# Decoder trunk with RWKV-7 mixing: the 16x16 eliminations go from VectorE to GpSimd, and each chain's blocks travel in 6 transfers instead of 20

## The chip, the cores and the metric

The kernel runs on 1 core of one Trainium2 chip. The metric is the device time of one execution in microseconds; of the kernel before there are three timed runs (median 1921.83, 1918.63 to 1923.67) and one profiled execution. A difference of about 0.3% is the least that a measurement of this kernel can tell from none.

## The reference, cut to what matters

Two layers; each layer is a SwiGLU feed-forward half step, a mixing step and another feed-forward half step. The mixing step concatenates sliding-window attention, RWKV-7 time mixing (4 heads of 64) and a short convolution. The part that matters here is the recurrence of RWKV-7 over 512 positions:

```python
def step(S, inp):
    r_t, w_t, k_t, v_t, kk_t, a_t = inp
    s_kk = jnp.einsum('bhvk,bhk->bhv', S, kk_t)
    S = (S * w_t[:, :, None, :] - s_kk[..., None] * (kk_t * a_t)[:, :, None, :]
         + v_t[..., None] * k_t[:, :, None, :])
    return S, jnp.einsum('bhvk,bhk->bhv', S, r_t)
```

## The kernel before, in words

Weights and activations are split into a high and a low half (`wH`/`wL`, `hnH`/`hnL`), and each large product is three matmuls. A weight tile is loaded through the SyncE queue (`wraw<-in_...`), cast on ScalarE (L101, `wH`) and subtracted on VectorE (L102, `wL`).

`mix` runs three things beside each other. `products` is the stream of projections `wmi` and then `wmo`, matmuls `ps_mm` at L98. `attention` is one generator. `rwkv(q)` is another, run for q = 0 and 1, two heads each; I call each run a chain, so there are four: two in each of the two layers. The loop at the end of `mix` takes product steps in between by the costs that the generators yield. The tile framework then orders the instructions of each engine from its own estimate of times; what it writes is fixed before the run, and each engine works its list strictly in order. So an instruction whose input is late holds back all that stands behind it on that engine.

Inside a chain the recurrence is computed in chunks of 64 positions. `pairs` makes `B` (matmuls `ps_c` at L824, mask on VectorE at L828). From `B`'s lower triangles the chain needs the inverse of 16 unit triangular 64x64 matrices (8 chunks, 2 heads). It is made in stages:

- The matrices are written to DRAM (`dl`, three transfers, L836 and L838), and the 64 diagonal blocks of 16x16 are read back with one block in each partition (`G`, eight transfers, L848).
- GpSimd sets `V_` (`inv`) to identity matrices (L850, L851). Then 15 elimination steps follow, each a product (L855, `elim`) and a difference (L856, `inv`) on VectorE: 30 instructions in a row that each need the one before, over 64 partitions and 15 to 64 elements of each (680 elements for the 15 products, and as many for the differences).
- The result goes to DRAM (`di`, one transfer, L858) and comes back spread over 128 partitions (`C`, eight transfers, L861).
- VectorE makes the block diagonal `T` from `C` (L915). TensorE transposes it (`ps_T`, L884), ScalarE copies that (`TT`, L919), and two levels of `ps_x`, `X` (L928), `ps_t` and `ps_tt` join the blocks to 64x64. Then come `ps_w`, `ps_gn` with `GT` and `N` (L965, L966) and the start state `St` (L969), `ps_o`, six sequential steps `ps_s` (L989, `St` at L990), `ps_ys`, `ps_v` and `ps_g`.

All transfers of a chain are issued from SyncE's queue, the one that also issues the weight loads, and it is worked in order too. GpSimd's queue holds the loads `wada` and the accumulating loads of the feed-forward parts; in `mix` it has nothing but memsets.

Of the kernel before, what the change touches and what calls it, by code (L numbers as in the profile page):

```python
# [8 lines left out]
F32 = mybir.dt.float32  # L9
# [3 lines left out]
ALU = mybir.AluOpType  # L13
# [3 lines left out]
P = 128  # L17
# [8 lines left out]
NB = T // P  # L26
CH = 64
NC = T // CH
HB = math.exp(-0.5) / 2
BASE = 16  # L30
# [27 lines left out]
def trunk_kernel(ctx, tc, ins, out, layers=L, phases=("ffn1", "mix", "ffn2")):  # L58
    nc = tc.nc
# [10 lines left out]
    dram = ctx.enter_context(tc.tile_pool(name="dram", bufs=1, space=bass.MemoryType.DRAM))  # L70
    tt, stt, ts = nc.vector.tensor_tensor, nc.vector.scalar_tensor_tensor, nc.vector.tensor_scalar
# [38 lines left out]
    rows = (slice(0, CH), slice(CH, P))  # L110
# [7 lines left out]
    for i in range(KD):  # L118
        t = hp_.tile([P, T], F32, name=f"h{i}")
# [15 lines left out]
    for name, v in (("eps", EPS), ("eps64", 64 * EPS), ("gneps", GN_EPS), ("nhb", -HB)):  # L135
        t = const.tile([P, 1], F32, name=f"v_{name}")
# [7 lines left out]
    def cst(name):  # L144
        a, b = CON[name]
        return con[:, a:b]
# [61 lines left out]
    def square(i, sl):  # L208
        sq = E("sq")[:, sl]
        act(sq, h[i][:, sl], AF.Square)  # L210
        return sq
# [373 lines left out]
    def mix(l, hn, ss, mp, then, ready):  # L585
# [5 lines left out]
        def pair(name):  # L591
            return rows_of(name != "y4", (name + "H", name + "L"))

        def S(q, name, shape=(P, T)):
            return mp.tile(list(shape), F32, name=f"{name}{q}", tag=f"s{q}", bufs=8)
# [4 lines left out]
        def EQ(q, name):  # L600
            return mp.tile([P, T], F32, name=name, tag=f"e{q}", bufs=2)
# [154 lines left out]
        def rwkv(q):  # L756
# [38 lines left out]
            t = EQ(q, "k2")  # L795
# [36 lines left out]
            B_, other = yield from pairs(be, "B", other)  # L832
            LT = B_[:, :, :, 0]

            dl = dram.tile([P, 2 * NB, CH], F32, name="dl", tag=f"dl{q}", bufs=2)
            nc.sync.dma_start(dl[rows[0]], LT[rows[0]].rearrange("p e b t -> p (e b) t"))  # L836
            for e in range(2):
                nc.sync.dma_start(dl[rows[1], (1 - e) * NB : (2 - e) * NB], LT[rows[1], e])  # L838
            NM = CH // BASE
            NT = 2 * NM * 2 * NB  # L840
            square = lambda t: t[:NT, : BASE * BASE].rearrange("p (t u) -> p t u", u=BASE)
            G = square(EQ(q, "G"))
            for c in range(2):
                for m in range(NM):
                    n = (c * NM + m) * 2 * NB
                    p0 = c * CH + m * BASE
                    src = dl[p0 : p0 + BASE, :, m * BASE : (m + 1) * BASE]
                    nc.sync.dma_start(G[n : n + 2 * NB], src.rearrange("r n t -> n r t"))  # L848
            V_ = square(EQ(q, "inv"))
            nc.gpsimd.memset(V_, 0.0)  # L850
            nc.gpsimd.memset(V_.rearrange("p t u -> p (t u)")[:, :: BASE + 1], 1.0)  # L851
            for s in range(BASE - 1):
                n = BASE - 1 - s
                t = mp.tile([NT, BASE * BASE // 4], F32, name="elim", tag=f"el{q}")[:, : n * (s + 1)].rearrange("p (t u) -> p t u", u=s + 1)
                tt(t, G[:, s, s + 1 :].unsqueeze(2).to_broadcast([NT, n, s + 1]), V_[:, s : s + 1, : s + 1].to_broadcast([NT, n, s + 1]), ALU.mult)  # L855
                tt(V_[:, s + 1 :, : s + 1], V_[:, s + 1 :, : s + 1], t, ALU.subtract)  # L856
            di = dram.tile([2 * NM, 2 * NB, BASE, BASE], F32, name="di", tag=f"di{q}", bufs=2)
            nc.sync.dma_start(di.rearrange("m n t u -> (m n) t u"), V_)  # L858
            C_ = EQ(q, "C")[:, : 2 * NB * BASE].rearrange("p (n u) -> p n u", u=BASE)
            for m in range(2 * NM):  # L860
                nc.sync.dma_start(C_[m * BASE : (m + 1) * BASE], di[m].rearrange("n t u -> t n u"))  # L861


            AX = U(q, "AX", [P, 2, NB, 2, CH])
# [48 lines left out]
            T4 = T_.rearrange("p e b (m u) -> p (e b) m u", u=BASE)  # L913
            msk = cst("diag").rearrange("p (m u) -> p m u", u=BASE).unsqueeze(1).to_broadcast([P, 2 * NB, NM, BASE])
            tt(T4, C_.unsqueeze(2).to_broadcast([P, 2 * NB, NM, BASE]), msk, ALU.mult)  # L915
# [39 lines left out]
            with tc.manual_schedule(engines={mybir.EngineType.PE}):  # L955
                for b in range(NB):
                    for c, e in ce:
                        m = mm(pgs[c][rows[e], 0, b], Wn[rows[c], c ^ e, b, :CH], beN[rows[c], b, rows[e]], start=True, stop=True)
# [12 lines left out]
            y = S(q, "y")  # L971
            pos = [psum([P, 2, NB, CH], "ps_o", R) for _ in range(2)]
            with tc.manual_schedule(engines={mybir.EngineType.PE}):
                for b in range(NB):
                    for c, e in ce:
                        m = mm(pos[c][rows[e], 0, b], Wn[rows[c], c ^ e, b, :CH], B_[rows[c], e, b, 1], start=True, stop=True)
# [116 lines left out]

        prod = products()
        live, waiting = {}, {"rwkv0": lambda: rwkv(0), "rwkv1": lambda: rwkv(1), "att": attention}
        left, fill, credit = 2 * RWKV_WORK + ATT_WORK, FILL_WORK, 0.0
        more = True
# [28 lines left out]
        for q in range(2):  # L1126
            x = pair("yr")
# [256 lines left out]
```

## Time and profile before

| what | value |
|---|---|
| median of 3 timed runs | 1921.83 us |
| profiled execution, its own time | 1921.27 us |
| its span in the profile | 1919.3 us |
| PE (TensorE matmul) busy | 1876.9 us, 98% |
| DVE (VectorE) busy | 1395.9 us, 73% |
| ACT (ScalarE) busy | 847.0 us, 44% |
| POOL (GpSimd) busy | 130.7 us, 7% |
| elimination steps on DVE | 60 and 60 instructions, 11.4 and 11.4 us busy |

Times in the trace are in microseconds from the start of the span. The first layer's mixing stands between about 435 and 620, the second layer's between about 1375 and 1560; an instruction of the second layer's mixing comes about 941.3 us after its twin of the first layer (the first `dl` store starts at 476.66 and at 1417.98). In a row of the timeline the first two numbers are start and duration, and the brackets at its end say how long the engine had been idle and what ended that. "SPq" is the time that SyncE's queue takes to issue transfers, not the transfers themselves. Matmuls of float32 stand twice in the trace and once in the orders below.

### The profile page before, as it was taken

The page shows a single profiled execution, that of the slowest core. Times are in us where ns is not written, and L with a number is a line of the kernel's source. Part 1 is how long each engine was busy: PE and PEld are TensorE (multiplying, and loading weights), DVE is VectorE, ACT ScalarE, POOL GpSimd, SP SyncE. Part 2 cuts the span into 40 slices and gives each one's busy share as a digit, 9 for nine tenths or more (in the row PEclk, how much of TensorE's full clock was granted, in tenths as well). Part 3 has the DMA queues.
Part 4 walks back from the last instruction along what each step waited for, and adds up shares of the span by engine and source line. Part 5 has one row for each costly group of instructions (what it writes and reads, how often), then busy time and mean ns, then how long its engine had stood idle before and what let it go on. Part 6 is the DMA issues. An engine that isn't in the chain of part 4 may idle for free. (4 is left out here: it accounts for less than half of the span.)

```text
span 1919.3 us, 37594 instructions
## 1 busy us (share of the span) xinstructions
PE 1876.9 (98%) x15744; PEld 1737.6 (91%) x15744; DVE 1395.9 (73%) x2185; ACT 847.0 (44%) x1292; POOL 130.7 (7%) x212
## 2 busy tenths in 40 slices
PE   8999999999999999999999999999998999999999
PEld 7998899987789999899899988989877899988998
DVE  7687687758966877677877776876598668873862
ACT  4443355356432554155345514544563335532551
POOL 0101101000000001110100020010000000110000
PEclk8999999999999999999999999999999999999999
DMA  7767877421312476887726687781211215764741
GB/s 299 252 163 228 261 195 241 153 69 47 86 39 75 124 196 181 272 218 200 259 79 179 169 272 227 197 276 44 89 55 49 87 34 156 213 213 134 197 139 59
DMA packets 104457, 308.50 MB, mean 161 GB/s; under 512 B 23520, under 2 KB 24544, under 8 KB 103264
## 3 DMA queue, kind: packets, MB, share of 16 engines
q1 hardware_dynamic: 76064, 203.33, 32.3%
q0 software_dynamic: 28224, 102.77, 21.5%
q8 instruction: 123, 2.02, 0.4%
q14 instruction: 46, 0.38, 0.1%
HBM read 302.66 MB, written 3.41 MB: 159 GB/s over the span
## 5 line engine op out<-in xcount | busy, mean ns | idle before, releaser
L101 ACT CAST wH<-wraw 128x1024 fp32r<-128x1024 f32 (+2 forms) x292 | 268.2, 922 | 512.0 <-PE ps_mm L91 162.0
L102 DVE TENSOR_TENSOR wL<-wraw,wH 128x1024 fp32r<-128x1024 f32 (+2 forms) x292 | 308.3, 1059 | 97.1 <-ACT wH L101 96.3
L90 PE MATMUL ps_mm<-actH,wH 128*128 128x512 f32 (+1 forms) x784 | 288.5, 368 | 0.0
L91 PE MATMUL ps_mm<-actL,wH 128*128 128x512 f32 (+1 forms) x784 | 288.0, 367 | 0.0
L92 PE MATMUL ps_mm<-actH,wL 128*128 128x512 f32 (+1 forms) x784 | 288.0, 367 | 0.0
L441 PE MATMUL ps_d<-comH,wH 128*128 128x256 f32 x816 | 226.7, 278 | 1.4 <-ACT wH L101 0.8
L443 PE MATMUL ps_d<-comH,wL 128*128 128x256 f32 x816 | 225.7, 277 | 2.3 <-DVE wL L102 2.3
L442 PE MATMUL ps_d<-comL,wH 128*128 128x256 f32 x816 | 225.4, 276 | 0.0
L98 PE MATMUL ps_mm<-hnH,wH 128*128 128x256 f32 x1040 | 215.9, 288 | 5.0 <-ACT hnH L101 2.9
L98 PE MATMUL ps_mm<-hnL,wH 128*128 128x256 f32 x1040 | 213.9, 284 | 0.0
L98 PE MATMUL ps_mm<-hnH,wL 128*128 128x256 f32 x1040 | 209.1, 282 | 0.5 <-DVE wL L102 0.5
L163 DVE SCALAR_TENSOR_TENSOR wada<-wada,crep 128x1024 f32<-128x1024 f32 x140 | 168.1, 1220 | 55.9 <-DMA wada<-in_wadaT 55.7
L102 DVE TENSOR_TENSOR wL<-sum,wH 128x1024 fp32r<-128x1024 f32 x102 | 124.9, 1224 | 73.7 <-ACT wH L101 73.6
L98 PEld LDWEIGHTS ps_mm<-hnH,wH 128*128 128x128 f32 x1040 | 160.8, 191 | 16.3 <-issue 7.9
L92 PEld LDWEIGHTS ps_mm<-actH,wL 128*128 128x128 f32 x784 | 147.8, 189 | 24.3
L91 PEld LDWEIGHTS ps_mm<-actL,wH 128*128 128x128 f32 x784 | 147.8, 189 | 24.2
L90 PEld LDWEIGHTS ps_mm<-actH,wH 128*128 128x128 f32 x784 | 147.8, 189 | 24.2
L98 PEld LDWEIGHTS ps_mm<-hnL,wH 128*128 128x128 f32 x1040 | 161.4, 191 | 7.1 <-issue 6.2
L101 ACT CAST wH<-sum 128x1024 fp32r<-128x1024 f32 x102 | 107.5, 1054 | 136.5 <-PE ps_d L442 60.1
L98 PEld LDWEIGHTS ps_mm<-hnH,wL 128*128 128x128 f32 x1040 | 160.2, 191 | 4.7 <-issue 3.4
L441 PEld LDWEIGHTS ps_d<-comH,wH 128*128 128x128 f32 x816 | 153.3, 188 | 3.5 <-ACT wH L101 1.4
L443 PEld LDWEIGHTS ps_d<-comH,wL 128*128 128x128 f32 x816 | 153.2, 188 | 2.9 <-DVE wL L102 2.9
(404 smaller groups left out, 4238.1 us busy)
## 6 DMA issues: line engine op xcount, KB each, us to landing
wada<-in_wadaT POOLq DMA_DIRECT2D x128, 512.0 KB, 4.9
wraw<-in_wmi SPq DMA_DIRECT2D x40, 512.0 KB
wraw<-in_w2p SPq DMA_DIRECT2D x36, 512.0 KB
wraw<-in_w1p SPq DMA_DIRECT2D x32, 512.0 KB
wraw<-in_w1o SPq DMA_DIRECT2D x32, 384.0 KB
wraw<-in_w2o SPq DMA_DIRECT2D x32, 384.0 KB
wraw<-in_w1i SPq DMA_DIRECT2D x20, 512.0 KB
wraw<-in_w1o SPq DMA_DIRECT2D x32, 320.0 KB
```

The lines of the kernel that those rows point to most:

```text
L90: mm(acc, wH, xH, start=start, stop=False)
L91: mm(acc, wH, xL, start=False, stop=False)
L92: mm(acc, wL, xH, start=False, stop=stop)
L98: mm(acc[:, sl], w[a][:, k], x[b][:, sl], start=start and n == 0 and sl is HALVES[0], stop=stop and n == 2, skip_group_check=True)
L101: nc.scalar.copy(hi, src)
L102: nc.vector.tensor_sub(lo, src, hi.bitcast(F32))
L163: stt(w, w, 1.0, crep, ALU.mult, ALU.mult, accum_out=out_)
L441: mm(pt[:, i], wH, x[k][0], start=start and i + k == 0, stop=False, skip_group_check=True)
L442: mm(pt[:, i], wH, x[k][1], start=False, stop=False, skip_group_check=True)
L443: last = mm(pt[:, i], wL, x[k][0], start=False, stop=k == 3, skip_group_check=True)
```

## The change

The 30 elimination instructions of each chain are issued on GpSimd instead of VectorE, with the same shapes. The layout of `dl` is changed so that all 64 blocks are read back into `G` by one transfer instead of eight, and that of `di` so that one transfer brings `C` instead of eight. The two memsets, the three `dl` stores and the `di` store stay. The new lines from L842 on are 4 or 5 lower than the old ones.

```diff
-            dl = dram.tile([P, 2 * NB, CH], F32, name="dl", tag=f"dl{q}", bufs=2)
-            nc.sync.dma_start(dl[rows[0]], LT[rows[0]].rearrange("p e b t -> p (e b) t"))
+            dl = dram.tile([2 * NB * 2, CH * CH + CH], F32, name="dl", tag=f"dl{q}", bufs=2)
+            dv = dl[:, : CH * CH].rearrange("(n c) (r t) -> c r n t", c=2, t=CH)
+            nc.sync.dma_start(dv[0], LT[rows[0]].rearrange("p e b t -> p (e b) t"))
             for e in range(2):
-                nc.sync.dma_start(dl[rows[1], (1 - e) * NB : (2 - e) * NB], LT[rows[1], e])
...
+                nc.sync.dma_start(dv[1][:, (1 - e) * NB : (2 - e) * NB], LT[rows[1], e])
             G = square(EQ(q, "G"))
-            for c in range(2):
-                for m in range(NM):
-                    n = (c * NM + m) * 2 * NB
-                    p0 = c * CH + m * BASE
-                    src = dl[p0 : p0 + BASE, :, m * BASE : (m + 1) * BASE]
-                    nc.sync.dma_start(G[n : n + 2 * NB], src.rearrange("r n t -> n r t"))
+            nc.sync.dma_start(G, dl.rearrange("x (m z) -> (x m) z", m=NM)[:, : BASE * CH].rearrange("y (r t) -> y r t", t=CH)[:, :, :BASE])
...
-                tt(t, G[:, s, s + 1 :].unsqueeze(2).to_broadcast([NT, n, s + 1]), V_[:, s : s + 1, : s + 1].to_broadcast([NT, n, s + 1]), ALU.mult)
-                tt(V_[:, s + 1 :, : s + 1], V_[:, s + 1 :, : s + 1], t, ALU.subtract)
-            di = dram.tile([2 * NM, 2 * NB, BASE, BASE], F32, name="di", tag=f"di{q}", bufs=2)
-            nc.sync.dma_start(di.rearrange("m n t u -> (m n) t u"), V_)
+                nc.gpsimd.tensor_tensor(t, G[:, s, s + 1 :].unsqueeze(2).to_broadcast([NT, n, s + 1]), V_[:, s : s + 1, : s + 1].to_broadcast([NT, n, s + 1]), ALU.mult)
+                nc.gpsimd.tensor_tensor(V_[:, s + 1 :, : s + 1], V_[:, s + 1 :, : s + 1], t, ALU.subtract)
+            di = dram.tile([2 * NB, 2 * NM, BASE, BASE], F32, name="di", tag=f"di{q}", bufs=2)
+            nc.sync.dma_start(di.rearrange("n m t u -> (n m) (t u)"), V_.rearrange("p t u -> p (t u)"))
             C_ = EQ(q, "C")[:, : 2 * NB * BASE].rearrange("p (n u) -> p n u", u=BASE)
-            for m in range(2 * NM):
-                nc.sync.dma_start(C_[m * BASE : (m + 1) * BASE], di[m].rearrange("n t u -> t n u"))
+            nc.sync.dma_start(C_, di.rearrange("n m t u -> (m t) n u"))
```

The framework orders everything around the chains anew. On TensorE, first layer, chain 0, before: the first `ps_T` stands among the `ps_c` of chain 1, long after `ps_kk` of chain 1.

```order
L824 MATMUL ps_c<-AR_6004,iP_5948 64x128 x9
L884 MATMUL ps_T<-con,T_5307 64x64 x16
L824 MATMUL ps_c<-AR_6004,iP_5948 64x128 x4
L884 MATMUL ps_x<-T_5307,B_5115 64x64
L824 MATMUL ps_c<-AR_6004,iP_5948 64x128
L884 MATMUL ps_x<-T_5307,B_5115 64x64 x15
L824 MATMUL ps_c<-AR_6004,iP_5948 64x128 x2
L869 MATMUL ps_vN<-con,v_5768 128x128 x4
```

The same place of the chain now: `ps_T` stands just ahead of `ps_kk` of chain 1, 21 products behind the last attention product `ps_av`.

```order
L98 MATMUL ps_mm<-hnL,wH 128x256 x2
L98 MATMUL ps_mm<-hnH,wL 128x256
L879 MATMUL ps_T<-con,T_5293 64x64 x16
L98 MATMUL ps_mm<-hnH,wL 128x256
L611 MATMUL ps_kk<-kksq,con 128x512
L879 MATMUL ps_x<-T_5293,B_5115 64x64 x16
L98 MATMUL ps_mm<-hnH,wH 128x256 x2
```

So `ps_T` of chain 0 has moved from the place that TensorE reached at 523.17 in the trace of before to the one just ahead of `ps_kk`, which it reached at 503.04. In the second layer it stands even earlier, directly behind that `ps_av`, without the 21 products.

On VectorE, first layer, before, around chain 1's reciprocal (L791): elimination steps of chain 0 alternate with other work.

```order
L855 TENSOR_TENSOR elim<-G,inv 64x60
L785 COPY pc_5943<-P_5934 128x8
L791 RECIPROCAL iP_5948<-P_5934 128x512
L856 TENSOR_TENSOR inv<-inv,elim 64x6x10
L635 SCALAR_TENSOR_TENSOR gd<-ps_mm,par,gd 128x511
L855 TENSOR_TENSOR elim<-G,inv 64x55
L788 TENSOR_SCALAR rn<-ps_kk 128x512
```

The same place now: `T`, which needs `C`, stands directly behind the reciprocal, ahead of a weight split.

```order
L785 COPY pc_5929<-P_5920 128x8
L791 RECIPROCAL iP_5934<-P_5920 128x512
L910 TENSOR_TENSOR T_5293<-C,con 128x512
L635 SCALAR_TENSOR_TENSOR gd<-ps_mm,par,gd 128x511
L810 TENSOR_TENSOR AR_5990<-r_5676,P_5920 128x512
L102 TENSOR_TENSOR wL<-wraw,wH 128x1024
```

The elimination is gone from VectorE, and what waits for `C` now holds back the rows below it. In the second layer `T` stands two scans (L783) ahead of the reciprocal.

SyncE's queue, second layer, before: `G` is read after one weight load, `di` and `C` much later.

```order
L838 DMA dl<-B_15845 64x4x64
L836 DMA dl<-B_15845 512x1x64
L838 DMA dl<-B_15845 64x4x64
L267 DMA wraw<-in_wmi 128x1024
L848 DMA G<-dl 8x16x16 x8
L267 DMA wraw<-in_wmi 128x1024 x2
L1010 DMA gw<-in_gw 128x256
L267 DMA wraw<-in_wmi 128x1024
L267 DMA wraw<-in_wmo 128x768
L858 DMA di<-inv 64x256
L861 DMA C<-di 16x8x16 x8
```

The same place now: `G` stands behind two weight loads, and `di` and `C` ahead of the next ones.

```order
L842 DMA dl<-B_15817 64x4x64
L840 DMA dl<-B_15817 64x8x64
L842 DMA dl<-B_15817 64x4x64
L267 DMA wraw<-in_wmi 128x1024 x2
L844 DMA G<-dl 64x16x16
L854 DMA di<-inv 64x256
L267 DMA wraw<-in_wmi 128x1024
L856 DMA C<-di 128x8x16
L1005 DMA gw<-in_gw 128x256
L267 DMA wraw<-in_wmi 128x1024
```

One weight load moved ahead of `G`, and one now stands between `di`, which waits for GpSimd, and `C`. In the first layer that third load stands ahead of `di`.

On GpSimd the 30 instructions of a chain stand directly behind its two memsets, each waiting for the one before; ahead of the very first one stands one more instruction (L851, ISA), which loads the code library. TensorE's order is the same again from chain 1's `ps_t` of the first level on, in both layers.

More of the change, by code (lines that the diff above doesn't have):

```diff
@@ L833, in rwkv @@
             LT = B_[:, :, :, 0]
-            dl = dram.tile([P, 2 * NB, CH], F32, name="dl", tag=f"dl{q}", bufs=2)
-            nc.sync.dma_start(dl[rows[0]], LT[rows[0]].rearrange("p e b t -> p (e b) t"))
+            NM = CH // BASE
+            NT = 2 * NB * 2 * NM
+            square = lambda t: t[:NT, : BASE * BASE].rearrange("p (t u) -> p t u", u=BASE)
+            dl = dram.tile([2 * NB * 2, CH * CH + CH], F32, name="dl", tag=f"dl{q}", bufs=2)
+            dv = dl[:, : CH * CH].rearrange("(n c) (r t) -> c r n t", c=2, t=CH)
+            nc.sync.dma_start(dv[0], LT[rows[0]].rearrange("p e b t -> p (e b) t"))
             for e in range(2):
[L838 to L841, printed above, removed]
+                nc.sync.dma_start(dv[1][:, (1 - e) * NB : (2 - e) * NB], LT[rows[1], e])
             G = square(EQ(q, "G"))
-            for c in range(2):
-                for m in range(NM):
-                    n = (c * NM + m) * 2 * NB
-                    p0 = c * CH + m * BASE
-                    src = dl[p0 : p0 + BASE, :, m * BASE : (m + 1) * BASE]
-                    nc.sync.dma_start(G[n : n + 2 * NB], src.rearrange("r n t -> n r t"))
+            nc.sync.dma_start(G, dl.rearrange("x (m z) -> (x m) z", m=NM)[:, : BASE * CH].rearrange("y (r t) -> y r t", t=CH)[:, :, :BASE])
             V_ = square(EQ(q, "inv"))
```

## The prediction

> **What bounds the kernel now.** I read the page's busy times first, then the windows of the first layer's mixing, then who TensorE waits for there, then the timeline of the chain's steps.
>
> ```profile
> PE 1876.9 (98%) x15744; PEld 1737.6 (91%) x15744; DVE 1395.9 (73%) x2185; ACT 847.0 (44%) x1292; POOL 130.7 (7%) x212
> ```
>
> TensorE is busy nearly throughout, so the change can only win what TensorE idles around the chains. Columns of the windows: length, then PE, PEld, DVE, ACT and POOL busy.
>
> ```profile
> 480.00:500.00 20.00, 19.15 (x210) 14.71 (x208) 17.04 (x59) 11.27 (x34) 0.00 (x0) 1.00 0.34 97
> 500.00:520.00 20.00, 19.79 (x179) 18.07 (x178) 20.00 (x37) 7.32 (x9) 0.43 (x2) 1.00 0.18 52
> 520.00:540.00 20.00, 16.63 (x468) 14.36 (x466) 15.93 (x49) 6.28 (x15) 0.00 (x0) 1.00 0.25 60
> 540.00:560.00 20.00, 18.26 (x314) 15.55 (x314) 11.65 (x24) 4.02 (x9) 0.00 (x0) 0.91 0.12 29
> ```
>
> While VectorE is full (500 to 520), TensorE loses 0.2 us; it loses 3.4 and 1.7 us in the two windows after, where VectorE is not full. So a lighter VectorE gains nothing by itself; what counts is which wait ends last. The waits of TensorE in the second layer's mixing (total, times, longest):
>
> ```profile
> PE ps_o L976 <- DVE St L969: 2.6, 1, 2.6
> PE ps_s L989 <- ACT y L984: 1.8, 1, 1.8
> PE ps_T L884 <- DVE T L915: 1.3, 2, 0.9
> ...
> PE ps_x L884 <- ACT TT L919: 0.6, 2, 0.3
> ```
>
> **What goes.** 120 elimination instructions leave VectorE:
>
> ```profile
> L856 DVE TENSOR_TENSOR inv<-inv,elim 64x15 f32<-64x15 f32 (+7 forms) x60 | 11.4, 190 | 1.1
> L855 DVE TENSOR_TENSOR elim<-G,inv 64x15 f32<-64x15 f32 (+7 forms) x60 | 11.4, 189 | 1.1
> ```
>
> In chain 0 they stand between other work, from 490.52 to 513.98. In chain 1 they run back to back and block `GT`, whose `ps_gn` is done long before:
>
> ```profile
> 490.52 0.16 DVE L855 TENSOR_TENSOR elim<-G,inv 64x15 f32<-64x15 f32 x1
> ...
> 513.98 0.15 DVE L856 TENSOR_TENSOR inv<-inv,elim 64x15 f32<-64x15 f32 x1
> ...
> 532.83 0.16 DVE L855 TENSOR_TENSOR elim<-G,inv 64x15 f32<-64x15 f32 x1
> ...
> 539.59 0.17 DVE L856 TENSOR_TENSOR inv<-inv,elim 64x15 f32<-64x15 f32 x1
> 539.68 0.41 DVE L965 TENSOR_TENSOR GT<-ps_gn,con 128x256 f32<-128x256 f32 x1
> ```
> ```profile
> 536.66 0.29 PE L963 MATMUL ps_gn<-AX,beN 64*64 64x64 f32 x8
> 541.24 0.34 PE L976 MATMUL ps_o<-B,AX 64*64 64x64 f32 x8 [2.55 <-DVE St L969]
> ```
>
> The 30 steps take 539.68 - 532.83 = 6.9 us, 0.23 us each. Without them `GT`, `N` and `St` (1.5 us) follow `ps_gn` at once, and the 2.55 us go in both layers. The fourth chain's wait for `C` costs 0.9 us more: 2 x 2.55 + 0.9 = **6.0 us to win**. The new order puts more products between the steps of the inverse, which shortens the small waits (such as `ps_x`, 0.3 us each), but changes between products and small matmuls 7 to 9 times more per layer; I set these against each other.
>
> **What comes: `T` is due much earlier.** TensorE now meets chain 0's `ps_T` 21 products after `ps_av` (first layer), or right after it (second).
>
> ```profile
> 499.30 1.03 PE L1087 MATMUL ps_av<-pmp,V 128*64 128x512 f32 x4
> ...
> 503.04 0.59 PE L611 MATMUL ps_kk<-kksq,con 128*128 128x512 f32 x1
> ```
> ```profile
> 500.33 3.35 DVE L791 RECIPROCAL iP<-P 128x512 f32<-128x512 f32 x1
> 503.60 0.15 DVE L856 TENSOR_TENSOR inv<-inv,elim 64x60 f32<-64x60 f32 x1
> ```
>
> The 23 products between `ps_av` and `ps_kk` took 2.7 us, so `ps_T` is due at about 502.8 in the first layer. VectorE gets to `T` behind the reciprocal, 1 to 2 us before 503.6 since 19 steps ahead of it are gone. So `C` must be there by 502.0. In the second layer (its times less 941.3) `ps_T` is due at 500.2, so `C` by 499.5. Every us later is a us of TensorE: on VectorE the weight split `wL` is queued behind `T`, on TensorE everything behind `ps_T`.
>
> When is `C` there? The queue of SyncE (start, time to issue):
>
> ```profile
> 479.02 0.64 SPq L838 DMA_DIRECT2D dl<-B  x1
> 480.28 0.34 SPq L267 DMA_DIRECT2D wraw<-in_wmi  x1
> 481.12 3.02 SPq L848 DMA_DIRECT2D G<-dl  x8
> 484.23 8.01 SPq L267 DMA_DIRECT2D wraw<-in_wmi  x2
> 492.33 0.38 SPq L1010 DMA_DIRECT2D gw<-in_gw  x1
> 508.13 0.33 SPq L267 DMA_DIRECT2D wraw<-in_wmi  x1
> 512.63 0.33 SPq L267 DMA_DIRECT2D wraw<-in_wmo  x1
> 514.19 0.48 SPq L858 DMA_DIRECT2D di<-inv  x1
> ```
> ```profile
> 1463.91 0.63 SPq L838 DMA_DIRECT2D dl<-B  x1
> ...
> 1466.51 3.14 SPq L848 DMA_DIRECT2D G<-dl  x8
> 1481.18 0.46 SPq L858 DMA_DIRECT2D di<-inv  x1
> 1483.70 5.12 SPq L861 DMA_DIRECT2D C<-di  x8
> ```
> ```profile
> 1490.54 0.69 DVE L915 TENSOR_TENSOR T<-C,con 128x512 f32<-128x512 f32 x1 [1.43 <-DMA C<-di]
> ```
>
> - The last piece of `C` was issued by 1488.82 and `T` began at 1490.54: 1.7 us from issue to use. `di` to the first `C` took 2.5 us.
> - `G` now follows a second weight load; it is issued near 481.9 (its `dl` had landed by 481.1). One transfer instead of eight takes between one eighth of 3.0 us and all of it to issue, then 1.7 us, and lies behind 1 MB of weights: 484 to 487, I take 486.3. Before, `G` was not waited for at all, since VectorE came to it at 490.5.
> - `C` takes between 0.5 and 5.1 us to issue, then 1.7. I take 3.0 in all.
> - So `C` is there at 486.3 + 30c + 2.4 + 3.0 = 491.7 + 30c, with c the time of one step on GpSimd.
>
> The third weight load, now between `di` and `C` in the second layer, puts 0.8 us of its own ahead of that `C`; its own delay is covered, since in the trace the next load comes 16 us later (492.2 to 508.1).
>
> For chain 1, `ps_T` stands behind `ps_o` to `ps_g` (541.24 to 553.72 before, 12.5 us) and then 42 to 59 products and four groups of small matmuls, so about 22 us after the second half of `B` in the first layer and 21 in the second, where `B` comes later:
>
> ```profile
> 553.72 1.02 PE L1012 MATMUL ps_g<-gd,gw 128*128 128x512 f32 x2
> ```
>
> It needs 3.2 for `dl` (0.6 to issue one, then 2.6 from the last one's issue at 1463.91 to `G`), 2.7 for `G`, 30c, 5.4 for `di` and `C` and 0.7 for `T`: 12.0 + 30c. A chain is late when c is over 0.34, 0.23 (chains 0), 0.33, 0.30 (chains 1).
>
> **The disputed price is c.** The trace has no two-input GpSimd instruction; its nearest rows are memsets, the second waiting for the first:
>
> ```profile
> 468.17 0.30 POOL L850 MEMSET inv<- 64x256 f32 x1 [76.90 <-DVE es L1055]
> 468.53 0.12 POOL L851 MEMSET inv<- 64x16 f32 x1
> ```
>
> 0.18 us for 240 more elements is 0.77 ns each; 0.36 us from start to start leaves 0.16 us fixed. A step has 1360 / 30 = 45 elements, so as cheap as a memset c is 0.20. Twice VectorE's 0.23 is 0.47. I take 0.35, near the middle and above the memsets, since two inputs must be read. Then the chains are late by 0.3 and 3.6 us, and 0.6 and 1.5: **6.0 us to lose**. Profiled time 1921.3 - 6.0 + 6.0 = 1921.3; the median of the runs lies 0.5 higher, so 1922. At 0.20 nothing is late: -6.0. At 0.47: 30 x (0.13 + 0.24 + 0.14 + 0.17) = 20.4 late, +14.4.
>
> The Trainium skill (GPSIMD Engine Reference, "Performance versus the Vector engine") gives a two-input GpSimd operation about 2.6 cycles of 1.2 GHz per element and calls it the wrong engine for such work. 45 elements are then 98 ns, and with the memsets' 0.16 us c is an estimate of 0.26, by which the sum would be -5; no run shows it yet.
>
> **Rivals.**
>
> - *GpSimd is quick enough* (c up to 0.24, or the denser order gains more than I grant). For it: 0.20 by the memsets, and 468.7 to 486 as a free stretch for GpSimd to get ready. Against: a read must come on top. Time: 1921.8 - 6 = 1916, to 1913 with a better order.
> - *GpSimd's steps wait for VectorE's* (slower). Both engines work on SBUF at once, and chain 0's steps now fall where VectorE is full. If a step can't start while VectorE reads two inputs, each weight split of 1.2 us and each 512-wide product of 0.7 us holds the chain: 3 us in a chain, c in effect 0.45, late by 30 x (0.11 + 0.22 + 0.12 + 0.15) = 18 us, so 1922 + 12 = 1934; it decides from an effective c of 0.40 on. Against: VectorE's inputs are often in PSUM there.
>
> ```profile
> 490.61 1.21 DVE L102 TENSOR_TENSOR wL<-wraw,wH 128x1024 fp32r<-128x1024 f32 x1
> ```
>
> The Trainium skill (SBUF — State Buffer, "Who interferes with whom") says just this: a VectorE instruction with two SBUF inputs and a GpSimd instruction that reads SBUF exclude each other for a whole instruction. The trace of before, with GpSimd idle there, can't show it.
>
> - *The first step of all waits for its code.* One library load stands behind the first memsets; if it runs there, it hides in 468.7 to 486. If it delays the first step instead, chain 0 of the first layer alone pays, once, all of it as wait at `ps_T`; from 5.8 us on it decides: 1928 or later. The Trainium skill (GPSIMD Engine Reference, "Instruction dispatch") puts the first call after a load at about 6 us, which would be just that.
> - *It doesn't matter*: TensorE makes up for it elsewhere. That is within the forecast.
>
> **Chances.** Forecast (within 0.3%, 5.8 us, about what a measurement of this kernel can tell from none; c between 0.24 and 0.40): 0.37. Quick GpSimd: 0.27. Steps held or c over 0.40: 0.29. Code load: 0.07, on the slower side. So faster 0.27, same 0.37, slower 0.36. The range goes from 1913 to 1937 (c = 0.47, +14.4).
>
> **What would show it.** On GpSimd, 30 steps at 0.35 us from start to start, some 10.5 us; `ps_o` without its 2.55 us; a new wait of TensorE for `T` at `ps_T`, largest in chain 0 of the second layer (3 to 4 us); `T` on VectorE waiting for `C`. Wrong if `ps_T` waits nowhere, if the steps' pitch is outside 0.24 to 0.40, if steps stretch beside `wL`, or if TensorE's loss shows up elsewhere than at `ps_T` and `ps_o`.

## The result, and the profile after

The changed kernel takes 1925.47 us (median of 11 runs, 1922.49 to 1930.76); the kernel before takes 1920.58 in the 11 runs it is compared with (1915.38 to 1923.67). The ratio is 1.0033, with a 95% interval from 1.0020 to 1.0046: slower by a third of a per cent, at the edge of what I called no change (the medians alone differ by 4.9 us, 0.25%). The profiled execution took 1923.96 us, its span is 1922.1.

I measure the mixing on TensorE from its first `ps_c` to its first `ps_d`. In the first layer it took 206.6 us before and 203.4 after, in the second 209.8 and 216.2: 3.2 us won, 6.4 lost. (Outside the mixing the two profiled executions differ by 1.2 us at the start and 2.0 the other way between the layers, where the change touches nothing.)

The page of the changed kernel first, then its groups on GpSimd, then who TensorE waits for over the whole span (total, times, longest):

```profile
PE 1879.9 (98%) x15744; PEld 1738.6 (90%) x15744; DVE 1379.5 (72%) x2065; ACT 847.3 (44%) x1292; POOL 168.1 (9%) x332
```
```profile
L852 POOL TENSOR_TENSOR inv<-inv,elim 64x15 f32<-64x15 f32 (+7 forms) x60 | 19.9, 332 | 4.7
L851 POOL TENSOR_TENSOR elim<-G,inv 64x15 f32<-64x15 f32 (+7 forms) x60 | 17.3, 289 | 76.1 <-DMA G<-dl 71.7
```
```profile
PE ps_T L879 <- DVE T L910: 11.6, 4, 5.2
```

The two waits of 2.55 us at `ps_o` are gone, and in their place TensorE waits 11.6 us for `T` at `ps_T` in the four chains: 0.5 and 2.1 us in the first layer, 3.8 and 5.2 in the second. These are the second layer's two (chain 0, then chain 1), each with the last matmuls ahead of it:

```profile
1436.93 1.03 PE L1082 MATMUL ps_av<-pmp,V 128*64 128x512 f32 x4
1441.72 1.13 PE L879 MATMUL ps_T<-con,T 64*64 64x64 f32 x32 [3.76 <-DVE T L910]
...
1489.89 0.65 PE L864 MATMUL ps_kaN<-con,iP 128*128 128x128 f32 x4
1496.57 1.13 PE L879 MATMUL ps_T<-con,T 64*64 64x64 f32 x32 [5.20 <-DVE T L910]
```

The `ps_T` group itself is marked 1.13 us instead of the 0.69 that it takes elsewhere: it runs at half the clock. That is the part that the prediction left out. Windows of the changed kernel at that place; the number after the five busy times is the clock that TensorE was granted:

```profile
546.10:549.51 3.41, 1.47 (x13) 1.27 (x11) 1.26 (x2) 0.75 (x2) 0.00 (x0) 1.00 0.55 90
549.51:552.92 3.41, 3.22 (x77) 3.06 (x81) 0.04 (x1) 1.22 (x3) 0.00 (x0) 1.00 0.11 44
1436.95:1440.36 3.41, 1.01 (x6) 0.13 (x2) 0.00 (x0) 0.58 (x1) 0.00 (x0) 1.00 0.83 212
1440.36:1443.77 3.41, 2.05 (x36) 1.74 (x36) 2.85 (x5) 0.80 (x3) 0.00 (x0) 0.50 0.05 15
1443.77:1447.18 3.41, 3.41 (x41) 2.95 (x41) 3.36 (x5) 1.57 (x2) 0.00 (x0) 0.50 0.01 2
1447.18:1450.60 3.42, 3.42 (x43) 3.08 (x43) 2.46 (x5) 1.91 (x2) 0.00 (x0) 0.50 0.30 67
1450.60:1454.01 3.41, 3.41 (x51) 2.58 (x50) 1.79 (x3) 1.17 (x3) 0.00 (x0) 1.00 0.23 91
1491.56:1494.97 3.41, 0.00 (x0) 0.00 (x0) 0.00 (x0) 0.00 (x0) 0.00 (x0) 1.00 0.29 39
1494.97:1498.38 3.41, 1.81 (x35) 1.73 (x36) 0.69 (x1) 0.64 (x2) 0.00 (x0) 0.50 0.39 115
1498.38:1501.80 3.42, 3.42 (x24) 3.19 (x26) 0.00 (x0) 0.57 (x2) 0.00 (x0) 0.50 0.02 5
```

After a long wait the clock is at 0.50 for two or three stretches of 3.41 us. TensorE was busy for 2.05 + 3.41 + 3.42 + 1.81 + 3.42 = 14.1 us of that time and did half the work: 7.05 us lost, on top of the 9.0 us of waiting. The wait of 2.1 us in the first layer (first two rows) brought no such stretch. The same windows in the kernel before, at the `ps_o` waits of the two layers:

```profile
538.14:541.55 3.41, 0.86 (x26) 0.69 (x28) 2.81 (x13) 0.52 (x2) 0.00 (x0) 1.00 0.08 19
541.55:544.97 3.42, 3.42 (x96) 3.30 (x88) 0.76 (x2) 0.64 (x2) 0.00 (x0) 0.50 0.10 12
1480.22:1483.63 3.41, 1.06 (x71) 1.09 (x75) 2.17 (x10) 0.00 (x0) 0.00 (x0) 1.00 0.08 19
1483.63:1487.04 3.41, 3.41 (x51) 2.95 (x44) 0.97 (x3) 0.70 (x2) 0.00 (x0) 0.50 0.09 12
```

So each `ps_o` wait cost 2.6 + 1.7 us. Two more such times follow the small waits at the end of the mixings of before (3.41 us busy from 592.75, 6.09 us from 1534.83): 8.2 us lost in all before, 7.05 after. By layer, with the `ps_T` waits of before (0.4 and 1.3): in the first layer 2.6 + 0.4 + 3.4 = 6.4 before and 2.6 after, in the second 2.6 + 1.3 + 1.7 + 3.05 = 8.65 before and 9.0 + 7.05 = 16.05 after. The differences, -3.8 and +7.4, account for the measured -3.2 and +6.4 within 1 us.

### The profile page after: what moved, and what is told of

The parts are those of the page before. It is cut to its first block, busy times and chain, and to the rows that moved or that the text cites. A ratio compares the mean times of both kernels' runs of the same rounds, so it can differ in the third digit from the quotient of the medians.

```text
span 1922.1 us, 37494 instructions
## 1 busy us (share of the span) xinstructions
PE 1879.9 (98%) x15744; PEld 1738.6 (90%) x15744; DVE 1379.5 (72%) x2065; ACT 847.3 (44%) x1292; POOL 168.1 (9%) x332
## 3 DMA queue, kind: packets, MB, share of 16 engines
HBM read 302.66 MB, written 3.41 MB: 159 GB/s over the span
## 5 line engine op out<-in xcount | busy, mean ns | idle before, releaser
L98 PEld LDWEIGHTS ps_mm<-hnH,wH 128*128 128x128 f32 x1040 | 161.5, 192 | 14.1 <-issue 5.3
L92 PEld LDWEIGHTS ps_mm<-actH,wL 128*128 128x128 f32 x784 | 147.8, 188 | 24.4
```

Source lines behind the costliest of these rows:

```text
L92: mm(acc, wL, xH, start=False, stop=stop)
L98: mm(acc[:, sl], w[a][:, k], x[b][:, sl], start=start and n == 0 and sl is HALVES[0], stop=stop and n == 2, skip_group_check=True)
```

## The experiments

Times are medians, with the ratio to the runs of the kernel before on the same chip and its 95% interval. Waits and half-clock times are those of the one profiled run of each version; in experiments 1, 2, 6, 7 and 8 its time lies 5.7 to 8.6 us from the median, so such a number explains its own run and the median only in part.

**1. The transfers alone.** In the changed kernel, on both lines of the elimination:

```diff
-nc.gpsimd.tensor_tensor(...)
+tt(...)
```

> The 6 transfers per chain of the change, with all 120 elimination steps back on VectorE. My theory (the loss is TensorE's wait for T at ps_T, made by the longer chain over GpSimd, together with the half-clock time that follows a long wait): the order of the work is then that of before, ps_o keeps its two waits of 2.6 us, ps_T waits 0 to 1.7 us in all, as before; only the small wait for C goes: 1919 to 1921 us, 0 to 1.5 us under before. Rival 'the new transfers are the slow part' (one transfer of 1024 pieces lands later than eight small ones): the waits for C and G on VectorE grow by 2 us and more per chain, and the time is at or over that of the change, 1925 us. Rival 'GpSimd's steps slow VectorE down': 1920 us too, so this run does not speak on it.

1926.3 us, 1.0041 (1.0024 to 1.0058). My figure was wrong. The rival that had the right one expected longer waits for `G` and `C` on VectorE. The trace bears that out in part: chain 1's first step waits 2.1 us for `G` in each layer, where none waited before, and `T` waits for no `C`. `ps_T` waits 2.3 us in all. What grew on TensorE is the wait at `ps_o`, now for `N`:

```profile
PE ps_o L971 <- DVE N L961: 6.3, 2, 3.2
```

Chain 1's steps now take 10.2 us on VectorE, with other work between them, instead of 6.9 back to back. But that is 1.2 us more at `ps_o` than before, and the profiled run took 1917.7 us, no more than the kernel before: it doesn't show why the median is 8.6 us higher. The 12 runs spread widely, and their times go with the granted clock of the whole run: 1917.4 us at 0.996, 1932.2 at 0.989. So half-clock time (two stretches in the profiled run) is the likely loss of the others, as far as the mean clock tells; where it falls is not shown.

**2. GpSimd alone**: the kernel before, with `tt` replaced by `nc.gpsimd.tensor_tensor` on both lines.

> The elimination on GpSimd with the 20 transfers per chain of before. TensorE's order is that of the changed kernel but for a few products. My theory: T comes later by what the 8 transfers of G and the 8 of C cost over one each, 2.5 us and 4.7 us, so up to 7 us in each of four chains; ps_T waits 25 to 40 us instead of 11.6, and half-clock time comes on top: 1945 to 1965 us. Rival 'the transfers hide anyway and GpSimd's steps alone are the loss': 1925 us as the change. It shows whether the transfers had to change for the move to be bearable.

1918.72 us, 1.0002 (0.9989 to 1.0015): no slower than before; my expectation was off by 26 us and more. The premise on the order was wrong. `T` does come later, 505.60 - 498.18 = 7.4 us after the steps end instead of 4.3, but the scheduler, with 14 transfers more in each chain, also put `ps_T` later: 25 products and `ps_kk` stand ahead of chain 0's in both layers, where the change has 21 and none, and 43 ahead of chain 1's instead of 7. The wait of the second layer's chain 0:

```profile
1441.12 0.28 PE L98 MATMUL ps_mm<-hnL,wH 128*128 128x256 f32 x1
1442.82 0.69 PE L884 MATMUL ps_T<-con,T 64*64 64x64 f32 x32 [1.42 <-DVE T L915]
```

A chain that is longer (24.9 to 26.4 us from the last `dl` store to `T`, against 21.5 to 24.5 in the change) and waits less (3.5 us at `ps_T` in all): with that my theory that the length of the chain is the loss fell. The new one was that what counts is where the order puts `ps_T` against the true time of `T`.

**3. Only chain 1 on GpSimd**: in the changed kernel, on both lines,

```diff
-nc.gpsimd.tensor_tensor(...)
+(nc.gpsimd.tensor_tensor if q == 1 else tt)(...)
```

> The change with chain 0's steps back on VectorE; only chain 1's 30 steps run on GpSimd. TensorE's order is then that of before with T of chain 0 late. My theory: the two waits of 2.6 us at ps_o go, and with them the half-clock periods of 3.4 us behind them (1.7 us of work each); chain 1's T is due about as late as before, so ps_T waits 0 to 2 us each: 1910 to 1916 us. Rival 'a GpSimd elimination loses whatever stands around it' (steps 1.5 times as long, exclusion with VectorE): 1921 to 1926 us, ps_T of chain 1 waiting 4 us and more.

1913.28 us, 0.9975 (0.9962 to 0.9988), as expected: faster than both kernels. `ps_o` waits nowhere, `ps_T` 2.6 us in four waits, and neither mixing has any half-clock time (203.5 and 202.5 us).

**4. The chain's transfers from GpSimd's queue**: `nc.gpsimd.dma_start` for `G`, `di` and `C`.

> The change, with G, di and C issued by GpSimd instead of SyncE; the order of TensorE, VectorE and ScalarE is unchanged. G no longer stands behind weight loads, and C not behind one. My theory: in the chains 0 the first step starts 2 to 3 us earlier, in chain 1 of the second layer up to 2; ps_T's 11.6 us fall to 3 to 6 and the half-clock time behind them from 7 us of lost work to 0 to 4: 1911 to 1919 us. Rival 'GpSimd beside VectorE is the loss': steps and VectorE are as before the move, so 1925 us. Rival 'a transfer issued by GpSimd lands later': first step no earlier, ps_T's waits stay or grow, 1925 us or more.

1935.05 us, 1.0095 (1.0074 to 1.0115). The second rival had it: the transfers reach their users later.

```profile
482.68 0.85 POOL L844 DMA_DIRECT2D G<-dl  x1 [90.69 <-DVE wL L102]
...
487.56 0.20 POOL L851 TENSOR_TENSOR elim<-G,inv 64x15 f32<-64x15 f32 x1 [3.54 <-DMA G<-dl]
```

From the issue of `G` to the first step the four chains take 4.9, 3.8, 5.9 and 4.4 us here, and 4.8, 2.6, 4.5 and 3.6 from SyncE's queue in the change. `di` to `T` took 5.1 and 5.2 us in the first layer instead of 4.3. From the last `dl` store to `T` the chains are 1.0 to 3.7 us longer. `ps_T` waits 19.2 us instead of 11.6, and 8.9 us are lost at half clock in the mixings instead of 7.05.

**5. A later due time in the second layer.** `G` in 8 transfers again:

```diff
-nc.sync.dma_start(G, dl.rearrange(...)[:, :, :BASE])
+gsrc = dl.rearrange(...)[:, :, :BASE]
+for n in range(0, NT, 8):
+    nc.sync.dma_start(G[n : n + 8], gsrc[n : n + 8])
```

> The change with G in 8 transfers again (eight partitions each, from the new layout) and C in one. G lands no later for it: 7.0 us from the last dl to the first step with 8 transfers (second run), 7.4 with one. But the order differs in one place: in the second layer 21 products now stand ahead of chain 0's ps_T, as in the first layer, where the change has none. New theory (what costs is a ps_T that the order puts ahead of the true time of T, and above all the half clock that a wait of 2.5 us and more brings): ps_T's 11.6 us fall to 5 to 7, the waits of 3.8 and 5.2 us are under 2.5, the 7 us lost to the half clock fall to 0 to 2: 1913 to 1918 us. Rival 'the chain over GpSimd itself is the loss': 1925 us as the change. Rival 'more issues on SyncE cost': over 1925 us.

1922.8 us, 1.0021 (1.0009 to 1.0033). Half right: chain 0's wait in the second layer went from 3.8 to 0.5 us, as the 21 products said. But both chains 1 still have only 7 products between `ps_kaN` and `ps_T`, and wait 3.9 us each, with half clock behind. In the first layer that wait was 2.1 us in the change: chain 1's first step now comes 7.6 us after the last `dl` store instead of 6.5, and its steps took 11.5 us instead of 10.6. So eight transfers of `G` were not free there, as I had expected them to be.

**6. Filled waits.** Matmuls on constants ahead of the first `ps_T`, in the second layer:

```diff
+for _ in range(fill):
+    mm(pts[0], cst("ident"), con[:, : NB * w].rearrange("p (b c) -> p b c", b=NB), start=True, stop=True)
...
-flip(None)
+flip(None, 12 if l == 1 else 0)
```

> The change with 12 matmuls of 128x256 on constants (0.25 us each, 3 us in all) ahead of each chain's first ps_T in the second layer; they add work and no result uses them. They run while TensorE would stand idle for T (3.8 and 5.2 us there), so they delay nothing. Theory of the half clock: idle stretches of 0.8 and 2.2 us no longer bring half-clock periods; the 7 us of work lost in the trace of the change fall to 0 to 2: 1918 to 1921 us, although work was added. Rival 'only the length of the wait counts': 1925 us, or up to 1931 where the matmuls come at the wrong time.

1924.93 us, 1.0025 (1.0012 to 1.0038). In the profiled run (1918.47 us) no half-clock time is left in the mixings, and the mean clock of the runs rose from 0.992 to 0.9955; but the time fell by less than can be told. The set (two records for each matmul) took 5.45 us instead of 3.0, more than the wait that it should fill:

```profile
1488.01 5.45 PE L876 MATMUL ps_T<-con 128*128 128x256 f32 x24
1493.38 0.69 PE L881 MATMUL ps_T<-con,T 64*64 64x64 f32 x32
```

**7. Only chain 1 on GpSimd, with 20 transfers**: the third run's edit, in the kernel before.

> The kernel of before with chain 1's 30 steps on GpSimd, its 20 transfers kept; chain 0's steps on VectorE. TensorE's order is that of before but that chain 1's first ps_T stands 20 products earlier, among the ps_s. ps_o loses its two waits of 2.6 us, but T of chain 1 comes 3.4 us later (10.3 against 6.9 us of steps) and is asked for 2 to 5 us earlier: theory of the due time: ps_T of chain 1 waits 4 to 8 us in each layer, half-clock time behind it: 1920 to 1928 us, no gain, against 1913 us of the third run, where 23 products stand between kaN and that ps_T. Rival 'the transfers make no difference and moving chain 1 alone gives the gain': 1912 to 1915 us.

1925.24 us, 1.0043 (1.0028 to 1.0059), as the due time had it. The same move gains 0.25% in experiment 3 and loses 0.43% here, where chain 1's `ps_T` stands among the `ps_s`, and waits:

```profile
548.00 0.49 PE L884 MATMUL ps_T<-con,T 64*64 64x64 f32 x8 [5.47 <-DVE T L915]
```

In the second layer it waits 7.9 us. Of these waits 1.2 and 3.7 us are the chain's own length, which the 20 transfers make 24.3 and 26.8 us instead of 23.1; the rest is the place.

**8. `C` in 8 transfers**: in the changed kernel,

```diff
-nc.sync.dma_start(C_, di.rearrange("n m t u -> (m t) n u"))
+for m in range(2 * NM):
+    nc.sync.dma_start(C_[m * BASE : (m + 1) * BASE], di[:, m].rearrange("n t u -> t n u"))
```

> The change with C in 8 transfers again and G in one. The order of the second layer is that of the fifth run (21 products ahead of chain 0's ps_T); in the first layer 35 products stand ahead of it, 14 more than in the change. From the end of the steps to T took 7.2 to 8.6 us with 8 transfers of C (second run) and 4.3 to 5.2 with one. Theory: T is later by 3 us in each chain than in the fifth run, the due times are no later but for chain 0 of the first layer: ps_T waits 9 us more in all than there, with half-clock time behind it: 1925 to 1935 us. Rival 'C's transfers hide': as the fifth run.

1925.97 us, 1.0044 (1.0027 to 1.0062). `ps_T` waits 13.7 us against 8.7 in the fifth run, and the mixings have 7 stretches of half clock against 4. The later `C` is paid wherever the order gives it no room.

**9. Both chains due later**: the fifth run's kernel, and one line ahead of `T_`:

```diff
+if q == 1:
+    yield 2.0
```

The yield tells the planner of more work, so it emits more products there. TensorE's order changes in chain 1 alone.

> The fifth run's kernel with one line more: a yield ahead of chain 1's T, so that 42 products instead of 7 stand between its kaN and its first ps_T (35 x 0.117 us = 4.1 us); nothing else of TensorE's order ahead of it changes, all 120 steps stay on GpSimd. Theory of the due time: chain 1's waits of 3.9 us at ps_T in both layers fall to 0 to 0.5, and the half-clock time behind them (3.4 us of lost work in the trace of the fifth run, with 1.6 more behind it) goes; the products are moved, not added, so up to 1 us may come back in the small waits after them: 1922.8 less 7 to 11 us, 1911 to 1916 us. Rival 'the chain over GpSimd itself is the loss': the wait only moves, 1921 to 1924 us.

1907.1 us, 0.9954 (0.9941 to 0.9968): the fastest version, 0.5% under before, with all 120 steps on GpSimd. The second layer's chain 1 here, then in the change (the last `dl` store, `T` on VectorE):

```profile
1459.80 0.64 SPq L842 DMA_DIRECT2D dl<-B  x1
```
```profile
1483.29 0.69 DVE L914 TENSOR_TENSOR T<-C,con 128x512 f32<-128x512 f32 x1 [4.16 <-DMA C<-di]
```
```profile
1478.46 0.60 PE L866 MATMUL ps_kaN<-con,iP 128*128 128x128 f32 x4
1484.12 0.69 PE L881 MATMUL ps_T<-con,T 64*64 64x64 f32 x32
```
```profile
1471.38 0.64 SPq L842 DMA_DIRECT2D dl<-B  x1
```
```profile
1495.73 0.69 DVE L910 TENSOR_TENSOR T<-C,con 128x512 f32<-128x512 f32 x1 [7.20 <-DMA C<-di]
```

The chain is as long as in the change, 1483.29 - 1459.80 = 23.5 us against 24.4 (chain 0: 23.6 and 24.0 against 24.0 and 24.5; chain 1 of the first layer 23.3 against 21.5). It is only asked for later. `ps_T` waits 1.7 us in the whole span, no half-clock time is left in the mixings, and they take 201.2 and 201.8 us.

**10. A smaller fill**: 6 matmuls instead of 12.

> The sixth run with 6 matmuls instead of 12 ahead of each chain's first ps_T in the second layer. They took 0.45 us each there, 5.45 us a set, more than the waits of 3.8 and 5.2 us; 6 take 2.7 us and fit. Theory of the half clock: idle rests of 1.1 and 2.5 us, at most one half-clock period in the second layer's mixing, which took 216.2 us in the change and 214.0 with 12: now 209 to 212; time 1918 to 1921 us. Rival 'only the length of the wait counts': mixing of the second layer 216 us as in the change, 1925 us.

1922.14 us, 1.0036 (1.0022 to 1.0050); the second layer's mixing took 215.7 us, close to the rival's 216. A miss. A rest of 2.2 us of waiting was enough for two stretches of half clock:

```profile
1442.55:1445.96 3.41, 1.22 (x35) 0.80 (x34) 1.19 (x5) 0.00 (x0) 0.00 (x0) 1.00 0.48 118
1445.96:1449.37 3.41, 3.41 (x54) 2.61 (x46) 3.41 (x3) 0.65 (x2) 0.00 (x0) 0.50 0.01 2
```

That filling a wait pays is therefore not shown; that half-clock time follows idle time is.

**11. Only chain 0 on GpSimd**: the third run's edit with `q == 0`.

> The change with chain 1's steps back on VectorE; only chain 0's 30 steps run on GpSimd. Chain 0's order is that of the change (0 products ahead of ps_T in the second layer), chain 1's first ps_T stands 59 to 73 products behind kaN. Theory of the due time: chain 0's waits of 0.5 and 3.8 us and the half clock behind the second stay; chain 1's waits of 2.1 and 5.2 us and the 2.6 us lost behind the second go: 1914 to 1919 us. Rival 'chain 0 had no one waiting for it, so its move is the whole loss': 1925 us and more, with ps_T of chain 0 waiting 4 us in both layers.

1920.09 us, 1.0018 (1.0007 to 1.0029), 1 us over what I gave it. Chain 0 waits 3.9 us in the second layer, and the half clock behind that is there (10.2 us from 1441.72); in the first layer it does not wait. Chain 1's waits fell from 2.1 and 5.2 to 1.5 and 0.4 us, but a stretch of half clock follows the first of them (from 557.67) and another stands late in the second layer's mixing (from 1537.30), 1.7 us of lost work each, which I had not expected. `ps_o` waits nowhere, although chain 1's steps are on VectorE: in this order they stand spread among other work.

**12. The ninth run's line in the kernel before.**

> The kernel of before with the one line of the ninth run (the yield ahead of chain 1's T): all steps on VectorE, 20 transfers. Up to chain 1's first ps_T the order of TensorE is that of before, so ps_o's two waits of 2.6 us stay, with the half clock behind them; behind it the products stand more evenly among the small matmuls, which can take the half-clock periods at the end of each mixing (1.7 and 3.0 us of lost work in the trace of before) and some of the 1.1 and 1.8 us waits at ps_s. Theory (the gain of the ninth run is the move's, once T is due when it is there): 1915 to 1919 us, 0 to 4 under before. Rival 'the line alone makes the gain': 1907 to 1910 us, as the ninth run, and ps_o's waits do not matter.

1916.71 us, 0.9990 (0.9979 to 1.0001), as expected. `ps_o` still waits:

```profile
PE ps_o L978 <- DVE St L971: 5.1, 2, 2.5
```

The half-clock time late in the two mixings (1.7 and 3.05 us of lost work before) is gone in the profiled run. So the line without the move is worth 0.1%, at most 0.2% by its interval, and the line with the move and its transfers 0.46%. The line with the new transfers and the steps on VectorE was not run.

## Why the prediction was right, and where it was wrong

The forecast, no change because 6 us won at `ps_o` are lost at `ps_T`, gave the time and the place. Its terms were less good than its sum: that the sum came out is in good part luck. Some of the prediction's own signs of being wrong came true: steps that stretch beside `wL`, which makes the mean pitch 0.41 us in both chains 0, just over its 0.40, and a loss of TensorE beyond the waits at `ps_T` and `ps_o`.

- *What goes.* The two `ps_o` waits went, as forecast, and experiment 3 against 1, and 7 against the kernel before, each pair with chain 1's steps on another engine and the same transfers, show that they hang on these steps on VectorE in those orders (the eleventh run has an order without the wait). Their price was too low: a wait of 2.55 us also brought 1.7 us of half-clock loss. The row that I quoted for 540 to 560 already had a clock of 0.91, and I read past it.
- *The price c.* Forecast 0.35 us. Undisturbed it is 0.344: in the first layer's chain 1, 29 steps from start to start took 543.87 - 533.89 = 9.98 us. In the other three chains it is 0.39 to 0.41, by the next point. The estimate of 0.26 worked out with the Trainium skill (GPSIMD Engine Reference, "Performance versus the Vector engine") failed on its fixed part: the smallest steps, of 15 elements, already start 0.28 us apart, where the memsets' 0.16 and the Trainium skill's rate make an estimate of 0.19, while the 0.1 us more from 15 to 64 elements is close to what that rate gives.

```profile
533.89 0.21 POOL L851 TENSOR_TENSOR elim<-G,inv 64x15 f32<-64x15 f32 x1 [17.70 <-DMA G<-dl]
...
543.87 0.65 POOL L852 TENSOR_TENSOR inv<-inv,elim 64x15 f32<-64x15 f32 x1
```

- *Steps that wait for VectorE.* This rival was right as a mechanism, at somewhat under half the size that I gave it. GpSimd's steps in chain 0, and VectorE's instruction beside the longest:

```profile
491.51 0.29 POOL L852 TENSOR_TENSOR inv<-inv,elim 64x60 f32<-64x60 f32 x1
491.89 1.23 POOL L851 TENSOR_TENSOR elim<-G,inv 64x63 f32<-64x63 f32 x1
493.19 0.30 POOL L852 TENSOR_TENSOR inv<-inv,elim 64x63 f32<-64x63 f32 x1
```
```profile
491.75 1.21 DVE L102 TENSOR_TENSOR wL<-wraw,wH 128x1024 fp32r<-128x1024 f32 x1
```

  The step ends just behind `wL`, 0.94 us longer than its neighbours. The Trainium skill (SBUF — State Buffer, "Who interferes with whom") has just this exclusion, and the trace agrees. It made the four chains' steps 12.1, 10.6, 12.0 and 11.6 us long, 0.4 to 1.7 us of it by stretched steps, where I had set 3 for a chain. An estimate from these figures is that without them the four waits at `ps_T` would be some 7.7 us instead of 11.6, since 0.5, 0.4, 1.6 and 1.4 us of them would go. No run here removes the stretching alone.
- *The first step's code.* No delay: 487.86 to 488.14 is a usual pitch. Whatever the load took went into the 18 us that GpSimd was idle before, as the rival's counter-case said.

```profile
487.86 0.20 POOL L851 TENSOR_TENSOR elim<-G,inv 64x15 f32<-64x15 f32 x1 [18.04 <-DMA G<-dl]
488.14 0.22 POOL L852 TENSOR_TENSOR inv<-inv,elim 64x15 f32<-64x15 f32 x1
```

- *When `T` is due.* Chain 0 came out as forecast, 0.5 and 3.8 us late against 0.3 and 3.6, though in the first layer by errors that cancel in part: `T` began at 504.22, 2 us after my 502.2 for `C`. Of that, 1.2 us is no error of the chain, since everything in this trace comes 1.2 us later at that place (the last `dl` store at 480.25 instead of 479.02). Of the rest, `G` took 0.4 us more from its issue to the first step (4.8 us; the eight of experiment 2 took 4.9), the steps took 1.6 us more, and `di` and `C` 1.1 us less. TensorE came 1.7 us later than my 502.8, 1.2 of it by the same shift. Chain 1 was mis-sized: 2.1 and 5.2 us against 0.6 and 1.5. I had `ps_T` due 22 and 21 us after `B`'s second half, it was due 20.8 and 20.6 us after the store of that half began; and the chain of the second layer took 3 us more than the first's, with `G` behind a weight load and steps held.
- *Every microsecond late is one microsecond of TensorE.* This is the step that failed: a term was missing. The late `T` cost 9.0 us of waiting and 7.05 of half clock in the second layer, 1.8 us of TensorE for each microsecond late. What saved the forecast is that the same term was missing on the other side, where 5.1 us of waits at `ps_o` were worth 8.5; that is luck.
- *The rival that I did not have* is the one the experiments point to: that the 6 us at `ps_T` are no price of GpSimd, but of a static order that asks for `T` too early. The ninth run keeps the steps, the stretching and chains about as long, and its ratio to before is 0.9954 where the change's is 1.0033; against the fifth run (1.0021) it differs by the one line alone.

What stays open: why the runs of the first experiment spread by 15 us, whether a fill of the right size at the right place would pay, and how much of the ninth run's gain the new transfers and the line would give with the steps on VectorE.

## What to carry to other kernels

In this kernel, moving a dependent chain to a slower engine cost nothing once its consumer was asked for later (the ninth run). Under a scheduler that fixes the order from its own estimates, look first at what stands between the chain's start and its consumer, and move that by a line, before judging the engine. Price a wait of the bounding engine by its length and by the clock that it loses after it: read the granted clock in the windows behind each wait of the kernel before. And look at the order again when the number of transfers changes: with 20 in a chain 25 products and `ps_kk` stood ahead of chain 0's `ps_T`, with 6 it was 21 products or none. That the scheduler does this because it counts the transfers is my reading; no run shows its estimates.

## What the runs showed of the hardware

- In the mixings of these fourteen traces TensorE's clock fell to half 30 times, and the busy share of the 3.41 us before was 0.00 to 0.61 each time. Shares from 0.43 (the changed kernel from 546.10) to 0.58 (the fifth run from 1534.38) were followed by half clock in some places and not in others, shares of 0.62 and more never. It lasted one to four stretches of 3.41 us. A wait of 2.2 us was enough in the tenth run, one of 2.1 us was not in the changed kernel. The Trainium skill (TensorE: Matmul & The Clock Gate, "HAM oscillation — how this bites in real kernels") names idle gaps of over about 3.4 us; the runs differ from that, since waits of 2.2 and 2.55 us did it.
- A dependent GpSimd instruction on 64 partitions with two inputs starts 0.28 us after the one before at 15 elements and 0.37 to 0.39 at 64.
- One transfer of 64 KB in 64-byte pieces (`G`) reached its first user, which waited for it, 2.6 to 4.8 us after its issue in the four chains of the change; eight of an eighth each took 4.4 to 4.9 us from the first one's issue in the second run.
- A GpSimd step beside a VectorE instruction with two inputs in SBUF was held: 1.23 us instead of 0.29 beside a `wL` of 1.21 us.
